# Forty projections as 20 Strassen pairs of blocks, with LayerNorm, RG-LRU and SSD between the products

## The chip, the cores and the metric

The program runs on one core of a Trainium2 chip. The metric is device time in microseconds (us); the median of three runs of the kernel before is 1493.83 us (1492.61 to 1494.31). The engines of the core are named as in the profile: PE (TensorE, matrix products), PEld (its weight loads), DVE (VectorE), ACT (ScalarE), POOL (GpSimd) and SP (SyncE, whose queue SPq issues the DMAs of this kernel).

## The reference

One layer of a hybrid encoder, for 1,024 prompt tokens and 64 tokens of a second stream, 1,088 in all, all in float32:

```python
h = rms_norm(x, norm_pre);  proj = h @ w_in          # (1088 x 1024) @ (1024 x 10248)
u_a = rg_lru(conv4(lru_x)) * silu(lru_g)             # block-diagonal gates, scan over time
u_b = rms_norm(ssd(silu(conv4(xbc)), dt) * silu(z), ssd_norm)   # chunked state-space scan
u_c = silu(layer_norm(conv31(glu(cf_in)))) * silu(cf_g)
u_d = stick_breaking_attention(q, k, v) * silu(sb_g)
y_b = u_b @ w_down[b]                                # four times 512 -> 1024
m = sum_b sigmoid(merge_b) * y_b                     # merge: 4 x 1024 columns of proj
out = x + rms_norm(m @ w_out, norm_post)
```

The columns of `w_in` make 80 blocks of 128, and 8 columns for `dt`. 32 of the 80 blocks are the merge gates, 4 each are the gates of the RG-LRU (`C_LG`) and of the convolution module (`C_CG`).

## The kernel before, in words

All products keep float32 accuracy with three passes: each operand is split in a rounded part and its remainder (`hh`, `hl` for the activations, `w_hi`, `w_lo` for the weights), and hi·hi, hi·lo, lo·hi are summed in PSUM (`mm3`, L104 to L107). Activations lie with channels on the partitions and tokens along the row, in three pieces `SPL` of 256, 384 and 448 tokens. One block of the projection (`proj`, L176) is a load of 512 KB of weights, a split on ACT (L97) and DVE (L98), and for each piece 8 x 3 = 24 matmuls, so 72 per block, with an evacuation by the caller.

PE runs in the order of the program text. The other engines' queues are in order too, their order set by a scheduler from priorities (`tc.high_priority`). `Feed` is how matrix work is laid between the steps of something else: `feed.step(n)` issues n pieces of the projections in its queue.

The stages: norm and transposes of the input (to about 35 us); the first projections; attention in 68 units with four chunks of heads (115 to 587 us), between whose units the projections of the convolution module, of q, k, v and of 12 gate blocks are fed, the latter (`spill`, L309) with a sigmoid on ACT, a product on DVE and a store to DRAM; the RG-LRU (587 to 745 us), fed with its own and the SSD's blocks and their 4-tap convolutions; the LayerNorm of the convolution module (745 to 880 us); the SSD in 9 chunks of 128 tokens (880 to 1230 us). From the LayerNorm on, the feed holds `merge(bi)` for three of the four branches: per block of the gate 72 matmuls of the projection, a sigmoid (L689), 36 matmuls with `w_down` (`down`), product and sum on DVE (L698, L699). A chunk of the SSD (`first`, `second`, `third`, `fourth`) has five feed steps in its loop. Its result is split into `uoh`, `uol` and stored (L924, L925). The last branch in `order` is the SSD's own: its 8 gate blocks are projected from 1230 to 1334 us, its downs run to 1382 us, and then the product with `w_out`. The operands of the downs are loaded by `load_u` (L662), two transfers per piece.

## Time and profile before

| | |
|---|---|
| median of the runs | 1493.83 us |
| span of the profiled execution | 1490.9 us |
| PE busy | 1460.1 us (98%) |
| DVE busy | 921.1 us (62%) |
| ACT busy | 588.5 us (39%) |
| POOL busy | 118.9 us (8%) |
| DMA, mean over the span | 97 GB/s |

The profiled execution spans 1490.9 us from its first to its last instruction; the median of the device times is 2.9 us longer. Times inside the span are counted from its start. A matmul's duration is modelled and overlaps the next one; how long PE takes for a row of matmuls is read from their starts.

### The profile page before, as it was taken

The page shows a single profiled execution, that of the slowest core. Times are in us where ns is not written, and L with a number is a line of the kernel's source. Part 1 is how long each engine was busy: PE and PEld are TensorE (multiplying, and loading weights), DVE is VectorE, ACT ScalarE, POOL GpSimd, SP SyncE. Part 2 cuts the span into 40 slices and gives each one's busy share as a digit, 9 for nine tenths or more (in the row PEclk, how much of TensorE's full clock was granted, in tenths as well). Part 3 has the DMA queues.
Part 4 walks back from the last instruction along what each step waited for, and adds up shares of the span by engine and source line. Part 5 has one row for each costly group of instructions (what it writes and reads, how often), then busy time and mean ns, then how long its engine had stood idle before and what let it go on. Part 6 is the DMA issues. An engine that isn't in the chain of part 4 may idle for free.

```text
span 1490.9 us, 23008 instructions
## 1 busy us (share of the span) xinstructions
PE 1460.1 (98%) x9157; PEld 1360.5 (91%) x9157; DVE 921.1 (62%) x1379; ACT 588.5 (39%) x1000; POOL 118.9 (8%) x157
## 2 busy tenths in 40 slices
PE   6999999999999999999999999999999999999997
PEld 5898999999999998999999999999999999999885
DVE  6289589579769955677765554656655541019433
ACT  6323434443453344666644322333332332124211
POOL 0003212231221222000000000000000000000000
PEclk9999999999999999999999999999999999999999
DMA  6232212313212323454433354222621234113322
GB/s 209 75 87 63 72 61 68 103 44 89 92 46 87 98 87 109 138 117 107 116 124 116 110 169 142 82 68 83 196 78 57 75 88 148 51 43 113 99 85 71
DMA packets 103339, 144.17 MB, mean 97 GB/s; under 512 B 20800, under 2 KB 82112, under 8 KB 103232
## 3 DMA queue, kind: packets, MB, share of 16 engines
q1 hardware_dynamic: 103232, 142.71, 31.9%
q8 instruction: 72, 1.18, 0.3%
q14 instruction: 35, 0.29, 0.1%
HBM read 97.95 MB, written 40.53 MB: 93 GB/s over the span
## 4 chain that ended last, share of the span: by engine, by line
PE 87%; issue 6%; DVE 4%; DMA 1%; ACT 1%; POOL 1%; SPq 0%; DVEq 0%; POOLq 0%; ACTq 0%
PE pj L105 24%; PE pj L106 24%; PE pj L107 24%; PE pg L468 2%; PE pg L450 2%; PE pg L106 1%; PE pg L107 1%; PE pg L105 1%; DVE cvo L239 1%; PE pz L417 1%; PE pz L418 1%; PE pg L878 1%; PE pg L736 1%; PE pg L871 1%; DMA g_bc<-in_npre_dram 0%
## 5 line engine op out<-in xcount | busy, mean ns | idle before, releaser
L105 PE MATMUL pj<-hh,w_hi 128*128 128x384 f32 (+2 forms) x1920 | 637.6, 332 | 1.7 <-ACT hh L220 1.7
L106 PE MATMUL pj<-hl,w_hi 128*128 128x384 f32 (+2 forms) x1920 | 631.8, 329 | 1.8 <-DVE hl L221 1.8
L107 PE MATMUL pj<-hh,w_lo 128*128 128x384 f32 (+2 forms) x1920 | 631.5, 329 | 0.0
L105 PEld LDWEIGHTS pj<-hh,w_hi 128*128 128x128 f32 x1920 | 363.6, 189 | 16.6 <-issue 2.1
L106 PEld LDWEIGHTS pj<-hl,w_hi 128*128 128x128 f32 x1920 | 363.7, 189 | 14.4 <-DVE hl L221 2.6
L107 PEld LDWEIGHTS pj<-hh,w_lo 128*128 128x128 f32 x1920 | 363.5, 189 | 11.0
L98 DVE TENSOR_TENSOR w_lo<-w_raw,w_hi 128x1024 fp32r<-128x1024 f32 x96 | 117.5, 1224 | 226.9 <-ACT w_hi L97 226.7
L97 ACT ACTIVATE w_hi<-w_raw 128x1024 fp32r<-128x1024 f32 x96 | 101.7, 1060 | 281.7 <-PE pj L106 262.6
L239 DVE SCALAR_TENSOR_TENSOR cvo<-cbuf,p_t,cvo 128x1118 f32<-128x1118 f32 x120 | 165.6, 1380 | 2.1
L105 PE MATMUL pj<-uh,w_hi 128*128 128x384 f32 (+2 forms) x384 | 126.2, 329 | 0.0
L107 PE MATMUL pj<-uh,w_lo 128*128 128x384 f32 (+2 forms) x384 | 126.2, 329 | 0.0
L106 PE MATMUL pj<-ul,w_hi 128*128 128x384 f32 (+2 forms) x384 | 126.1, 328 | 0.0
L438 DVE TENSOR_TENSOR_SCAN fb<-fb,ones 128x128 f32<-128x128 f32 (+8 forms) x68 | 90.0, 1324 | 38.0 <-POOL fb L435 37.4
L435 POOL TENSOR_SCALAR_AFFINE_SELECT beta<-beta 128x128 f32<-128x128 f32 (+1 forms) x72 | 78.2, 1086 | 14.4 <-ACT beta L431 13.7
L698 DVE TENSOR_TENSOR sg<-pj,sg 128x256 f32<-128x256 f32 (+2 forms) x48 | 25.7, 535 | 84.9 <-PE pj L107 80.6
L689 ACT ACTIVATE sg<-pj 128x256 f32<-128x256 f32 (+2 forms) x72 | 33.7, 468 | 112.2 <-PE pj L107 112.0
L105 PEld LDWEIGHTS pj<-uh,w_hi 128*128 128x128 f32 x384 | 72.7, 189 | 2.3
L106 PEld LDWEIGHTS pj<-ul,w_hi 128*128 128x128 f32 x384 | 72.6, 189 | 2.2
L107 PEld LDWEIGHTS pj<-uh,w_lo 128*128 128x128 f32 x384 | 72.6, 189 | 2.2
L435 POOL TENSOR_SCALAR_AFFINE_SELECT fb<-fb 128x128 f32<-128x128 f32 (+1 forms) x72 | 38.2, 530 | 449.2 <-ACT fb L430 354.4
L439 DVE TENSOR_TENSOR beta<-beta,fb 128x128 f32<-128x128 f32 (+8 forms) x68 | 50.3, 740 | 4.3 <-POOL beta L435 0.7
L452 ACT ACTIVATE wT<-pg 128x512 f32<-128x512 f32 (+3 forms) x96 | 43.3, 485 | 18.1 <-PE pg L450 17.8
(313 smaller groups left out, 1683.0 us busy)
## 6 DMA issues: line engine op xcount, KB each, us to landing
w_raw<-in_win_dram SPq DMA_DIRECT2D x80, 512.0 KB, 3.7
w_raw<-in_wdn_dram SPq DMA_DIRECT2D x16, 512.0 KB, 3.6
xt<-in_x_dram SPq DMA_DIRECT2D x8, 512.0 KB, 10.5
xbc<-xs SPq DMA_DIRECT2D x8, 512.0 KB, 2.6
xb<-xbc SPq DMA_DIRECT2D x8, 512.0 KB, 4.9
w_raw<-in_wout_dram SPq DMA_DIRECT2D x8, 512.0 KB, 3.7
xr<-in_x_dram SPq DMA_DIRECT2D x8, 512.0 KB, 3.8
out_y_dram<-yo SPq DMA_DIRECT2D x16, 256.0 KB, 2.3
```

The source lines that it names most:

```text
L97: S.activation(hi, r3, AF.Copy)
L98: V.tensor_sub(lo, r3, hi.bitcast(FT))
L105: PE.matmul(out, ah, bh, start=first, stop=False)
L106: PE.matmul(out, ah, bl, start=False, stop=False)
L107: PE.matmul(out, al, bh, start=False, stop=last)
L239: V.scalar_tensor_tensor(out[:, :n], b[:, i:i + n], w[:, i:i + 1], out[:, :n], op0=OP.mult, op1=OP.add)
L435: G.affine_select(t_[s, 1024 - w:1024], t_[s, 1024 - w:1024], pattern=[[-1, w]], compare_op=OP.is_gt, fill=fill, base=0, channel_multiplier=1)
L438: V.tensor_tensor_scan(F[:, rev], F[:, rev], ones[:, 0:1].to_broadcast([128, n]), 1.0, OP.mult, OP.mult)
L439: V.tensor_tensor(B[:, L:1024], B[:, L:1024], F[:, L + 1:1025], op=OP.mult)
L450: PE.transpose(p[:, (j - j0) * 128:(j - j0 + 1) * 128], B[:, L + j * 128:L + (j + 1) * 128], ident)
L452: S.activation(wT[:, j0:j1, :], p[:, :(j1 - j0) * 128].rearrange("p (j c) -> p j c", c=128), AF.Copy)
L689: S.activation(sg[:, :n], p[:, :n], AF.Sigmoid)
```

## The change

Forty of the 80 blocks (the 8 gate blocks of convolution module and RG-LRU, and the 32 merge gates) are no longer projected one by one: two blocks make a `Pair`, and the product of their 2 x 2 arrangement (2 halves of the inner dimension, 2 halves of 544 tokens) is made with seven products in place of eight, after Winograd. The seven weight operands are sums of 512-wide quarter blocks made on POOL (L693, L694, L695, L702), each split by ACT and DVE; the seven activation operands `quad` are made once, after the attention, with additions on POOL (L601) and DVE. One product is 2 x 12 matmuls of 272 columns. Sums of products are made by accumulating in the same PSUM bank, by ACT copies (L725) and by DVE additions (L728) in `r`, and each quarter is stored to DRAM.

So the order of the program is another: the attention is fed with the 12 blocks that have short convolutions (8 of the SSD, 4 of the RG-LRU) in place of 12 gate blocks; then come 4 blocks for z, `quad` and `dt`; then the 140 products of the 20 pairs, and after each one step of the chain LayerNorm, RG-LRU, SSD; then all downs, whose gates are loaded from DRAM. The pieces `SPL` of the remaining blocks are 384, 384 and 320 tokens, of two V blocks as before.

```diff
-SPL = ((0, 256), (256, 384), (640, 448))
+SPL = ((0, 384), (384, 384), (768, 320))
...
-    extra = [spill(C_SZ + c, sz_d[:, c]) for c in range(4)] + [spill(C_LG + c, lg_d[:, c]) for c in range(4)]
-    extra += [spill(C_CG + c, cg_d[:, c]) for c in range(4)]
+    extra = [sx_chunk(c) for c in range(8)] + [lx_chunk(c) for c in range(4)]
...
+    def short_conv(chunk, state, tail_o, w, bias, dst, silu):
+        b = conv_buf(cp, WA, KA, state, "abuf", bufs=1)
...
+            conv(xc, b, NA, KA, w, bias, first=True)
+            if silu:
+                sg = cp.tile([128, NA], FT, name="sg", tag="abuf", bufs=1)
+                S.activation(sg, xc[:, :NA], AF.Sigmoid)
+                V.tensor_tensor(xc[:, :NA], xc[:, :NA], sg, op=OP.mult)
...
+    ORDER = (1, 2, 6, 5, 7, 3, 4)
+    BANK = {1: "a", 6: "a", 7: "a", 4: "a", 2: "b", 5: "c", 3: "c"}
...
+                G.tensor_tensor(s1, a21, a22, op=OP.add)
+                G.tensor_tensor(s2, s1, a11, op=OP.subtract)
+                G.tensor_tensor(a21, a11, a21, op=OP.subtract)
...
+            for j in ORDER:
+                hi, lo = weights()
...
+                for q in range(2):
...
+                            PE.matmul(p, a_[:, k], b_[:, k, s], start=new and k == 0 and z == 0, stop=k == 3 and z == 2,
+                                      skip_group_check=True)
+                    with tc.high_priority(offset=C_PRIO):
+                        if to:
+                            S.activation(R[to][:, s], p, self.last if j == 4 else AF.Copy)
+                        else:
+                            r = R[{2: (0, 0), 7: (1, 1), 3: (0, 1)}[j]][:, s]
+                            V.tensor_tensor(r, p, r, op=OP.add)
...
+                between()
...
+    def chains():
+        yield from wait(15)
+        yield from layer_norm()
+        yield from lru()
+        yield from ssd()
...
+    for n, pair in enumerate(pairs):
...
+            next(side, None)
+        pair.run(next_weights, step)
+    while next(side, left) is not left:
+        pass
...
+    us = [load_u(0, ut, tag="u")]
+    nwd = weights(wdn[order[0], 0])
...
+    gates = [load_gate(order[0], d) for d in range(8)]
+    us += [load_u(1, hp, tag="hh"), load_u(2, hp, tag="hl")]
...
+        if bi == 1:
+            us.append(load_u(3, ut, tag="u"))
```

`layer_norm` goes through four quarters of 272 tokens, `lru` through 8 pieces of 544 tokens by one of four channel blocks, `ssd` through the 9 chunks; each `yield` hands over to one product. The chain waits 15 products, takes 23 for the LayerNorm, 34 for the RG-LRU and 77 for the SSD, 149 in all. Between two chunks of the SSD lie 8 products. What is left when the products end runs in the last loop. The tile `u0` (operands of the first downs) is in a pool on the right side, over the place of the SSD's tiles; `u1` and `u2` lie where `hh` and `hl` were, and the fourth lies in `u0`'s place.

**PE at the end of the SSD.** Before, the last chunk's state (L871), diagonal (L878) and state update (L886) stand between the matmuls of a down and those of a gate block (`Sb` is the state, `M` the decayed scores, `xdt` and `xdd` the inputs times dt, `pg` and `pj` are PSUM banks):

```order
L107 MATMUL pj<-uh_10224,w_lo 128x256
L871 MATMUL pg<-Sb_8590,xb 64x256 [waits DMAHW4_49,DMAHW3_49]
L871 MATMUL pg<-Sb_8590,xb 64x256
L878 MATMUL pg<-M_11417,xdt 64x64 [waits PE_49]
L878 MATMUL pg<-M_11417,xdt 64x64 x3
L878 MATMUL pg<-M_11418,xdt 64x64 x4
L886 MATMUL pg<-xdd,bt 64x128 [waits Activation_49]
L886 MATMUL pg<-xdd,bt 64x128 x3
L105 MATMUL pj<-hh_96,w_hi 128x384
```

After, from the same step (L955, L965, L974; L989 and L1000 are the transposes and the column sum of `join` and `norm`) to the first matmuls of the downs:

```order
L955 MATMUL pg_12633<-Sb_9644,xb 64x256 [waits DMAHW6_49,DMAHW5_49,Activation_49]
L955 MATMUL pg_12633<-Sb_9644,xb 64x256
L965 MATMUL pg_12638<-M_12576,xdt 64x64 [waits DVE_49,PE_49]
L965 MATMUL pg_12638<-M_12576,xdt 64x64 x3
L965 MATMUL pg_12638<-M_12581,xdt 64x64 x4
L974 MATMUL pg_12652<-xdd,bt 64x128 [waits DVE_49]
L974 MATMUL pg_12652<-xdd,bt 64x128 x3
L989 MATMUL pg_12663<-ident,yt 128x64 [waits DVE_49,PE_49]
L989 MATMUL pg_12663<-ident,yt 128x64 x3
L1000 MATMUL pg_12673<-yt,ones 128x64 [waits DVE_49,Activation_49]
L109 MATMUL pj_12767<-u_12692,w_hi 128x384 [waits DMAHW5_49,Activation_49]
L110 MATMUL pj_12767<-u_12692,w_hi 128x384 [waits DMAHW0_49]
```

What moved: no matmul of other work stands beside these steps any more. The 13 rows ahead of them, from the segment sums of chunk 8 (L912) on, stand behind the last product (L721) too, with no product among them.

**SP at the end of the SSD.** Before, the last stores (L924, L925) stand among the loads of operands of the last branch (L662), with weights (L92) behind:

```order
L662 DMA ul_11867<-ul_74 128x4x256 [waits DMAHW6_49,PE_49]
L662 DMA uh_11865<-uh_70 128x4x256 [waits PE_49]
L924 DMA uh_70<-uoh 512x1x64 [waits DMAHW0_49,Activation_49]
L925 DMA ul_74<-uol 512x1x64 [waits DMAHW1_49,DVE_49]
L662 DMA ul_11871<-ul_74 128x4x384 [waits DMAHW2_49,PE_49]
L662 DMA uh_11869<-uh_70 128x4x384 [waits DMAHW3_49,PE_49]
L92 DMA w_raw<-in_win_dram 128x1024 [waits DMAHW4_49,DVE_49]
L662 DMA uh_11873<-uh_70 128x4x448 [waits DMAHW5_49,DMAHW0_49,PE_49]
```

After, the last stores (L1009, L1010) stand behind the gates `sga` and most of `u1`, and the loads of `u0` (its tile number is 12692) behind them; the first waits for the landing of the second store:

```order
L1090 DMA u_12753<-ul_76 128x4x384 [waits DMAHW1_49]
L1009 DMA uh_73<-uoh 512x1x64 [waits DMAHW2_49,Activation_49]
L1010 DMA ul_77<-uol 512x1x64 [waits DMAHW3_49,DVE_49]
L1090 DMA u_12753<-ul_76 128x4x384 [waits DMAHW4_49]
L1090 DMA u_12692<-uh_75 128x4x384 [waits DMAHW3_49,DMAHW5_49,DMAHW2_49,PE_49]
L1090 DMA u_12692<-uh_75 128x4x384 [waits DMAHW6_49]
L1090 DMA u_12692<-uh_75 128x4x320 [waits DMAHW7_49]
L1090 DMA u_12692<-ul_79 128x4x384 [waits DMAHW0_49]
L1090 DMA u_12692<-ul_79 128x4x384 [waits DMAHW1_49]
```

What moved: the operands of the next matmuls, loaded around the SSD's last stores before, stand behind them.

**ACT in the RG-LRU.** Before, a weight split and an evacuation stand between the exponential (`ga`) and the hyperbolic tangent (`gr`):

```order
L620 ACT_TABLE_LOAD
L620 ACTIVATE ga<-gr,lm_6064 128x1092 [waits Activation_49]
L97 ACTIVATE w_hi<-w_raw 128x1024 [waits DMAHW1_49,PE_49]
L577 ACTIVATE abuf<-pj 128x384 [waits PE_49]
L577 ACTIVATE abuf<-pj 128x64
L621 ACTIVATE gr<-gr,lp_6065 128x1092 [waits Activation_49]
L622 ACT_TABLE_LOAD
L622 ACTIVATE gr<-gr 128x1092 [waits Activation_49]
```

After, the three functions and two weight splits stand in a row, ahead of two evacuations of a product (L725):

```order
L852 ACT_TABLE_LOAD [waits DMAHW4_49,DVE_49]
L852 ACTIVATE ga<-gr,lm_8102 128x544 [waits Activation_49]
L853 ACTIVATE gr<-gr,lp_8103 128x544 [waits Activation_49]
L854 ACT_TABLE_LOAD
L854 ACTIVATE gr<-gr 128x544 [waits Activation_49]
L228 ACTIVATE w_hi<-w_raw 128x512 [waits PE_49]
L228 ACTIVATE w_hi<-s_8335 128x512 [waits Pool_49]
L725 ACTIVATE r<-bank 128x272 [waits PE_49] x2
```

What moved: the evacuation that stood between the functions stands behind them and two weight splits.

## Rows read from the trace of the kernel before

**Rows 1.** The page: busy time of each engine, granted clock by slice, chain by engine.

```profile
PE 1460.1 (98%) x9157; PEld 1360.5 (91%) x9157; DVE 921.1 (62%) x1379; ACT 588.5 (39%) x1000; POOL 118.9 (8%) x157
...
PEclk9999999999999999999999999999999999999999
...
PE 87%; issue 6%; DVE 4%; DMA 1%; ACT 1%; POOL 1%; SPq 0%; DVEq 0%; POOLq 0%; ACTq 0%
```

**Rows 2.** Timeline of PE, a projection: start us, us, engine, line, operation, tiles, count.

```profile
1262.92 0.28 PE L105 MATMUL pj<-hh,w_hi 128*128 128x256 f32 x1
...
1265.79 0.34 PE L105 MATMUL pj<-hh,w_hi 128*128 128x384 f32 x1
...
1269.96 0.36 PE L105 MATMUL pj<-hh,w_hi 128*128 128x448 f32 x1
...
1274.91 0.28 PE L105 MATMUL pj<-hh,w_hi 128*128 128x256 f32 x1
```

**Rows 3.** PE's matmuls by form: count | busy us, mean ns | idle.

```profile
L105 PE MATMUL pj<-uh,w_hi 128*128 128x256 f32 x128 | 36.2, 283 | 0.0
...
L418 PE MATMUL pz<-kl,qs 128*128 128x320 f32 x16 | 4.8, 306 | 0.0
...
L105 PE MATMUL pj<-uh,w_hi 128*128 128x384 f32 x128 | 43.0, 336 | 0.0
```

**Rows 4.** Busy us of each engine by stretch, then granted clock, DMA share, GB/s.

```profile
215.00:341.00 126.00, 125.81 (x875) 117.86 (x873) 101.00 (x119) 54.63 (x115) 28.06 (x36) 1.00 0.24 74
880.00:1230.00 350.00, 348.43 (x2230) 328.35 (x2229) 196.06 (x373) 119.98 (x164) 0.00 (x0) 1.00 0.35 103
579.50:583.00 3.50, 3.20 (x22) 2.90 (x24) 1.26 (x4) 1.19 (x2) 2.04 (x5) 0.51 0.13 37
590.00:600.00 10.00, 10.00 (x60) 9.55 (x60) 3.94 (x18) 3.51 (x7) 0.00 (x0) 1.00 1.03 299
```

**Rows 5.** Timeline of VectorE at the end of the SSD.

```profile
1220.94 0.41 DVE L905 TENSOR_TENSOR yz<-yz,pg 128x256 f32<-128x256 f32 x1
...
1226.11 0.54 DVE L918 RECIPROCAL rs__11767<-rs__11767 128x64 f32<-128x64 f32 x1
...
1226.69 0.87 DVE L920 SCALAR_TENSOR_TENSOR yz<-yz,p_t,rs__11767 128x64 f32<-128x64 f32 x4
...
1228.09 0.43 DVE L225 TENSOR_TENSOR uol<-yz,uoh 128x256 fp32r<-128x256 f32 x1 [0.53 <-ACT uoh L224]
```

**Rows 6.** Timeline of ScalarE at the end of the SSD.

```profile
1222.32 0.42 ACT L908 ACTIVATE yt<-yz 128x256 f32<-128x256 f32 x1 [3.13 <-DVE yz L906]
...
1224.20 1.28 ACT L917 ACT_TABLE_LOAD   x1
...
1227.64 0.42 ACT L224 ACTIVATE uoh<-yz 128x256 fp32r<-128x256 f32 x1 [1.84 <-issue]
```

**Rows 7.** Groups of single operations on VectorE and ScalarE by form.

```profile
L98 DVE TENSOR_TENSOR w_lo<-w_raw,w_hi 128x1024 fp32r<-128x1024 f32 x96 | 117.5, 1224 | 226.9 <-ACT w_hi L97 226.7
...
L225 DVE TENSOR_TENSOR uol<-yz,uoh 128x512 fp32r<-128x512 f32 x8 | 5.4, 679 | 0.0
...
L772 DVE RECIPROCAL lnr<-lnr 128x256 f32<-128x256 f32 x1 | 1.7, 1746 | 0.0
...
L224 ACT ACTIVATE uoh<-yz 128x512 fp32r<-128x512 f32 x8 | 5.0, 631 | 19.8 <-PE pg L878 19.8
```

**Rows 8.** DMA issues: operation, count, KB each, median us from issue to landing.

```profile
ul<-uol SPq DMA_DIRECT2D x8, 256.0 KB, 2.7
```

**Rows 9.** Timeline of ScalarE in the RG-LRU.

```profile
704.11 1.21 ACT L621 ACTIVATE gr<-gr,lp 128x1092 f32<-128x1092 f32 x1
705.34 1.28 ACT L622 ACT_TABLE_LOAD   x1
```

**Rows 10.** Groups on POOL: an affine select beside VectorE's work and one alone.

```profile
L435 POOL TENSOR_SCALAR_AFFINE_SELECT beta<-beta 128x128 f32<-128x128 f32 (+1 forms) x72 | 78.2, 1086 | 14.4 <-ACT beta L431 13.7
...
L85 POOL TENSOR_SCALAR_AFFINE_SELECT tri_le<-ones 128x128 f32<-128x128 f32 x1 | 0.3, 292 | 0.0
```

More of the change, by code (lines that the diff above doesn't have):

```diff
@@ new lines, in encoder_step, with spill, evac @@
+    tmp = a5.enter_context(tc.tile_pool(name="tmp", bufs=1, side="right", reuse_waits="tile"))
+    def spill(chunk, dst):
+        def evac(t0, n, p):
+            g = tmp.tile([128, NM], FT, name="t3", bufs=3)
+            S.activation(g[:, :n], p[:, :n], AF.Silu)
+            dma(dst[:, t0:t0 + n], g[:, :n])
+        yield from proj(chunk, evac)
+    feed.add(*(spill(C_SZ + c, sz_d[:, c]) for c in range(4)))
+    feed.step(1)
+    tlo, thi = slice(0, HT), slice(HT, T)
+    k0, k1 = slice(0, 4), slice(4, 8)
@@ new lines, in encoder_step @@
+    feed.step(2)
+    dtr = tmp.tile([16, T], FT, name="dtr")
+    for i, (t0, n) in enumerate(SPL):
+        p = pg()
+        for k in range(8):
+            for q, hx in enumerate((hh, hl)):
+                PE.matmul(p[:16, :n], wd2[:, k, :], hx[:, k, t0:t0 + n], start=k == 0 and q == 0, stop=k == 7 and q == 1)
+        S.activation(dtr[:, t0:t0 + n], p[:16, :n], AF.Copy)
+    feed.step(3)
+    pd = pg()
+    for i in range(9):
+        r = 128 if i < 8 else 64
+        PE.transpose(pd[:r, i * 16:i * 16 + 16], dtr[:, i * 128:i * 128 + r], ident[:16, :16])
@@ new lines, in stored, with done, wait @@
+    def stored(base, c, dst, func=None):
+        def done(e, f, r, last):
+            if func and not last:
+                S.activation(r, r, func)
+            dma(dst[:, c + e, f * HT:f * HT + HT], r)
+        return Pair(base + c, base + c + 1, done, func or AF.Copy)
+    pairs = [stored(C_CG, c, cg_d, AF.Silu) for c in (0, 2)] + [stored(C_LG, c, lg_d, AF.Silu) for c in (0, 2)]
+    pairs += [stored(C_MG, 2 * i, mg_d) for i in range(16)]
+    def wait(n):
+        for _ in range(n):
+            yield
@@ new lines, in chains, with ahead @@
+    def chains():
[3 more added lines that the diff above has]
+        yield from ssd()
+    ready = []
+    todo = [(p, j) for p in pairs for j in ORDER]
+    two = []
+    def ahead(n):
+        while todo and len(ready) < n:
+            p, j = todo.pop(0)
+            p.prepare()
+            if not two:
+                t_ = wp.tile([128, 8, 128], FR, name="w_hi"), wp.tile([128, 8, 128], FR, name="w_lo")
+                two.extend([t[:, k] for t in t_] for k in (k0, k1))
+            hi, lo = two.pop(0)
+            p.parts(j, hi, lo)
+            ready.append((hi, lo))
@@ new lines, in next_weights, with step @@
+    def next_weights():
+        ahead(3)
+        return ready.pop(0)
+    side = chains()
+    left = object()
+    for n, pair in enumerate(pairs):
+        count = [0]
+        def step(n=n, count=count):
+            count[0] += 1
+            ahead(2)
+            if count[0] == 2 and n + 1 < len(pairs):
+                pairs[n + 1].prepare()
+            next(side, None)
+        pair.run(next_weights, step)
+    while next(side, left) is not left:
+        pass
+    order = (3, 0, 2, 1)
@@ L927, in encoder_step @@
-    prev = None
-    feed.step(LNB)
-    for i in range(9):
-        ch = Chunk(i)
-        ch.first()
-        if prev:
-            prev.third()
-        feed.step(2)
-        if prev:
-            prev.fourth()
-        feed.step()
-        ch.second()
-        feed.step(2)
-        prev = ch
-    prev.third()
-    feed.step()
-    prev.fourth()
-    feed.drain()
-    p3.close()
-    b = order[3]
-    us = [load_u(b, i) for i in range(3)]
-    sgp = ctx.enter_context(tc.tile_pool(name="sgp", bufs=1, side="right", reuse_waits="tile"))
@@ L985, in encoder_step @@
+    put.close()
+    ut = ctx.enter_context(tc.tile_pool(name="op", bufs=1, side="right", reuse_waits="tile"))
+    gp_bc = ut.tile([128, D], FT, name="gp_bc")
     dma(gp_bc, ap(npost, 0, [[0, 128], [1, D]]))
```

879 lines of the change are left out of this document (472 added, 407 removed).

## The prediction

> **What bounds the kernel now.** I read the page's busy times and clock first. PE is busy 98% of the span, at nine tenths of the clock or more in every slice, and the chain that ended last is PE for 87% [rows 1]. So the time is the number of columns that PE streams, by their price, plus the few places where PE stands. Next the price: in the timeline of a projection, 24 matmuls of 256 columns run from 1262.92 to 1265.79, 24 of 384 to 1269.96, 24 of 448 to 1274.91 [rows 2], that is 0.120, 0.174 and 0.206 us from start to start, and 11.99 us for a block of 72. Then the stages: in one attention chunk (215 to 341) VectorE is busy 101.0 of 126.0 us, in the SSD 196.1 of 350.0 and ScalarE 120.0, while PE has 125.8 and 348.4 [rows 4]. So nearly nothing waits today, every microsecond that PE is spared counts, and every one that it is made to wait counts too. Last the place where the change takes PE's cover away, the end of the SSD [rows 5, 6, 8].
>
> **Fewer columns (the gain).** The forty blocks cost 40 x 11.99 = 479.6 us. The change makes 20 pairs x 7 products x 24 = 3,360 matmuls of 272 columns. No row has 272. The modelled durations of 256, 320 and 384 columns are 283, 306 and 336 ns [rows 3], which is 163 and 162 ns over the pitch of 256 and 384; so 320 has a pitch of 0.144, and 272, a quarter of the way from 256 to 320, has 0.126 to 0.127. I take 0.1265: 3,360 x 0.1265 = 425.0, so -54.6. Bounds from the rows on either side: 0.120 gives 403.2 (-76.4), 0.144 gives 483.8 (+4.2). The 38 blocks left, in pieces 384, 384, 320, cost 24 x (0.174 + 0.174 + 0.144) = 11.8 against 11.99: -7.3 together. The 32 downs have half the matmuls per block: -3.1. Sum -65.0.
>
> **The end of the SSD (the largest loss).** The steps after the last product were hidden: from 1218 to 1242 us matmuls of downs and gates lay beside them. The changed order has nothing beside them, so I add them up, from T0, the end of the last product. Segment sums and exponential with a table load (1.28 [rows 6]) 2.3. Join of chunk 7: transposes 0.3, two 512-wide VectorE operations at 0.68 [rows 7], Square 0.63 [rows 7], two folds 0.7: 3.3. Norm of chunk 7: ones matmul 0.3, table load 1.28 and root 0.4 [rows 6], reciprocal 0.95 (1.746 for 256 [rows 7]), four scalings 1.4 (half as wide they took 0.87 [rows 5]), `uoh` 0.63, `uol` 0.68 [rows 7]: 5.5. That is T0 + 11. `xdt` of chunk 8 takes the place of `uoh`, so it waits for the store: 2.7 [rows 8], T0 + 13.8; scaling 0.7, diagonal 1.1, `yz` 0.9: 16.5. Join of chunk 8, 64 wide: 0.41 for each of two operations [rows 5], Square 0.42 [rows 6], folds 0.5 and a transpose: 18.3. Its norm, read from 1224.20 (table load) to the end of `uol` at 1228.09 + 0.43 [rows 5, 6], 4.3 less a short wait for ScalarE's turn: T0 + 22.
>
> Then the loads. The first down needs `u0` high and low of the first 384 tokens; its six loads are issued behind the SSD's last store, and that store stands behind gates and `u1`, 2.8 MB in the queues. At 299 GB/s, the most that a stretch of the trace moved [rows 4], these take 9.3 us from about T0 + 18 on, so the stores land near T0 + 28 and `u1`'s next piece at 30. The first low piece is the fourth load: 2.95 MB, 9.9 us at 299, so PE has its second matmul near T0 + 41. PE's own small matmuls in that stretch, 4 us, were there before too: +37. It would be 25 if the queues were empty at T0 + 20 (store 2.7, two pieces at 299) and the chain two steps ahead; 50 if loads and stores shared half the rate. I take 37, the sum of the rows.
>
> **What follows an idle PE.** After PE stood idle from 577 to 579.5 its granted clock was 0.51 for 3.5 us [rows 4], the lower level (1.2 GHz), then full. An idle stretch of 30 us ends the same way: 1.8 us lost there, and about 1 for the two later pieces of `u0`: +3. Bounds 0 and 6.
>
> **Between the products.** Per quarter of the LayerNorm (5 products, 15.2 us, and two float32 sums, 0.9) VectorE has 7,072 elements in its own steps at 1.224 us per 1,024 [rows 7] = 8.5, a reciprocal of 272 at 1.8 [rows 7], five weight splits at 0.68, four or five additions of 0.43 [rows 5], overheads of 0.1 each: 16.1 of 16.1 us. Per piece of the RG-LRU (4 products and 12 gate matmuls, 13.7 us) ScalarE has three table loads of 1.28 [rows 6], four gates at 0.45, three functions and two splits of 544 at 0.66 (0.63 for 512 [rows 7]), four weight splits at 0.63 and 4 to 5 evacuations at 0.42 [rows 6]: 13.4 of 13.7. Two queues with nothing to spare: I put 1 us per quarter and 1 to 1.5 per piece, 14. The SSD has slack (VectorE 23 of 29.7 us per chunk by the same prices), less a `uoh` store that lands 0.8 us before `xdt` needs it: 5, and 2 at pair boundaries. Of this 21, some 12 us stood in 600 to 1230 before: so much do PE's starts there leave over their pitches, of which busy time, whose ends are modelled, shows 1.6 in the SSD [rows 4]. +9. Bounds 0 and 40.
>
> On POOL the changed kernel has four 512-wide additions per pair, which the trace lacks. An affine select of 128 columns took 0.29 us alone and 1.09 beside VectorE's work [rows 10], so 512 wide I bound it by 1.2 and 4.3 us: 5 to 17 of the 21 us of a pair, prepared a pair ahead, at no cost. The Trainium skill ("GPSIMD Engine Reference", 3.1 and the specifications in 1) gives about 2.6 cycles per element for an operation of two tensors, some 1.1 us here as an estimate, and says that the engine shares SBUF's interface with VectorE operations of two SBUF inputs. By that VectorE would lose up to 3.2 us per LayerNorm quarter, where it has none, and the sum would be 13 us higher. The slow selects beside VectorE agree with the sharing; which side pays, the rows of before show for POOL alone.
>
> **Attention.** Twelve blocks with convolutions add 3 operations of 1,092 (1.38 to 1.22, [rows 7] for 1,024) or some 4 us per block to VectorE, and 1.3 more for a SiLU, less the 1.6 of a gate block: 40 us in 470, so 111 of 126 us per chunk. VectorE keeps its cover; the buffer `abuf` is single, so a second such block in a row waits for the first's convolution, 3 PSUM banks (12 us) ahead. +5, bounds 0 and 15. The start of the products (PSUM pools change, first quarter operands): +1.
>
> **Sum.** 1490.9 - 65.0 + 37 + 3 + 9 + 5 + 1 = 1480.9; with the 2.9 us between span and median, 1483.8: 1484.
>
> **Rivals.** *ScalarE's queue bounds the RG-LRU* (slower than before). Two table loads, three functions and two weight splits in a row, 5.8 us, stand ahead of two evacuations. A bank is accumulated into again one product later, so PE has 3.0 to 4.5 us; what is past that, and the splits queued behind, PE waits. If PE stands for the row less half a product, 4.3 us in each of 8 pieces, that is 35 us: 1519 with the rest as above. It decides from 1.6 us per piece (13 us) on. For it: 13.4 of 13.7 us. Against: table loads and functions come when the gates are there, often with the evacuation already done; in the trace ScalarE waits for PE, not the other way.
>
> *Table switches cost double* (slower). In the RG-LRU a table load started 0.02 us after the tangent's end, 704.11 + 1.21 to 705.34 [rows 9]: no wait ahead of it. If each of the 24 loads in the 8 pieces had a wait of its own length ahead, ScalarE would need 13.4 + 3 x 1.28 = 17.2 of 13.7 us, +28: 1512. The Trainium skill ("ScalarE: Activation LUTs", What ACT_TABLE_LOAD costs) states that much: 1,283 ns and a drain of 1,380 ns for every switch. By that rule the time would be 1515, as an estimate; the trace agrees with the first figure and not with the second.
>
> *A shorter end.* The scheduler's order is no promise of when the queues empty: with gates and `u1` landed before chunk 8's stores, `u0` starts at T0 + 24 and needs only its first pieces: 20 us rather than 37, 1467.
>
> *The saving isn't there.* If 272 columns cost what 320 do, the products take 483.8 us, nothing is saved, and the time is 1542.
>
> **How the numbers follow.** The forecast 0.57; ScalarE's queue 0.18; double switches 0.04; shorter end 0.17; no saving 0.04. The forecast's own range is 1466 to 1502, mainly the end (25 to 50) and the products (9, up to 20). With the rivals, 8 in 10 lie between 1460 and 1517. A measurement of this kernel can tell about 0.2% (3 us). Faster by more, under 1490.8: 0.7 of the forecast and the shorter end, 0.57. Within: 0.2 of the forecast, 0.12. Slower: the rest, 0.31.
>
> **What would show it.** Right: 3,360 matmuls at 0.126 to 0.127 from start to start; one gap of PE of some 35 us, from about 1140 on in the new span (downs 189 us and the last product with the output, 108 us, behind it), ended by DMA of `u0`, with the half clock behind it; VectorE over 95% busy in the LayerNorm, ScalarE in the RG-LRU; nearly no gaps in the SSD. Wrong: gaps of 3 us and more in each RG-LRU piece ended by ScalarE, gaps ended by POOL at pair starts, a clock at the lower level in the products, or a last stretch of under 20 us.

## The result, and the profile after

The changed kernel takes 1519.49 us (median, 1519.28 to 1520.43) against 1494.0 in the same comparison: a ratio of 1.0174 with a 95% interval of 1.0162 to 1.0186, 25 us slower. The forecast was 1484 with a range up to 1517. One of the runs below, of the kernel with later loads, took 4903.67 us and is left out. The profiled execution spans 1518.6 us, 27.7 more than before. Three parts of the page of after, busy time, granted clock by slice and chain, answer to [rows 1]:

```profile
PE 1417.0 (93%) x9665; PEld 1352.7 (89%) x9665; DVE 1060.6 (70%) x1604; ACT 676.1 (45%) x1227; POOL 262.4 (17%) x245
...
PEclk9999999999999999999898999999999589999999
...
PE 43%; DVE 6%; DMA 4%; ACT 4%; issue 1%; SPq 0%; DVEq 0%; ACTq 0%
```

PE is busy 43.1 us less, since columns were saved. But the span holds 70.8 us more in which PE is not busy, PE's share of the chain is 43% where it was 87%, and one slice is at half the clock. PE's waits of after from 640 to 1240 us, by line and releaser (total, times, longest), say where PE stands. In before, 600 to 1230 holds 1.1 us of such waits; here it is 66:

```profile
PE pg L779 <- DVE lns L756: 14.9, 3, 6.7
PE pj L109 <- DMA u<-uh: 13.8, 1, 13.8
PE pg L965 <- DVE xdt L937: 8.0, 4, 5.5
PE pj L110 <- DMA u<-ul: 6.4, 1, 6.4
PE pg L1000 <- DVE yt L995: 6.3, 2, 3.6
PE pg L109 <- ACT bdah L228: 6.3, 1, 6.3
PE bank L721 <- ACT r L725: 3.0, 5, 1.1
```

The LayerNorm's column sums (L779) take 14.9, the first gate matmul of the RG-LRU (L109 by `bdah`) 6.3, and the rows with `u`, `yt` and most of `xdt` are the end of the SSD. Over the whole trace the waits with a releaser are 93.8 us, 22.3 before. By place: end of the SSD 35.1, LayerNorm 14.9, RG-LRU 10.5, SSD between products 4.1, start of the products 7.2, attention from 467 us on 5.0 (2.9 before); the rest is the head of the program, as before.

The windows of after, with PE's busy time (second figure), granted clock, DMA share and GB/s at the end of each row, answer to [rows 4]. The first is a stretch of products, the next three follow a wait of PE in the LayerNorm or at the start of the RG-LRU, the last three are the end of the SSD:

```profile
650.40:707.80 57.40, 57.39 (x457) 57.39 (x458) 21.68 (x38) 22.34 (x47) 14.71 (x11) 1.00 0.37 124
...
735.00:740.00 5.00, 3.51 (x13) 3.28 (x14) 2.93 (x5) 3.26 (x4) 0.00 (x0) 0.50 0.84 256
...
780.00:785.00 5.00, 4.47 (x23) 4.24 (x24) 2.74 (x3) 0.49 (x1) 0.17 (x1) 0.65 0.38 109
805.00:810.00 5.00, 4.95 (x22) 4.63 (x22) 0.88 (x7) 1.78 (x4) 0.00 (x0) 0.50 0.15 46
1174.40:1212.40 38.00, 9.25 (x56) 6.08 (x55) 14.62 (x35) 19.96 (x24) 0.00 (x0) 0.57 0.94 309
1212.40:1219.40 7.00, 0.62 (x2) 0.22 (x2) 0.00 (x0) 0.00 (x0) 0.00 (x0) 0.50 1.07 372
1219.40:1225.00 5.60, 5.60 (x20) 5.60 (x21) 0.56 (x1) 0.00 (x0) 0.00 (x0) 0.60 1.07 366
```

Three readings. 457 matmuls of 272 columns in 57.40 us are 0.1256 each, so 3,360 cost 422, where 425 was forecast. From the last product (1174.4) to the second matmul of the downs (1219.4) 45 us pass, with DMA at 0.94 to 1.07 of its engines. And PE ran at or near the lower clock level (1.2 GHz) behind waits in five places after the attention, not one: busy time times what is missing of the clock is 1.8, 1.6, 2.5, 4.0, 0.3 and 2.2 us in these rows, with 740 to 745 (0.74) and 620 to 625 (0.50) 2.7 more, 15 us in all. Summed in stretches of 5 us over the whole trace it is 18.2, against 2.7 before, so 15 to 16 are new. Without it PE's busy time would have fallen by 58, not 43. So the account is -58 for PE's work at full clock, +15 for clock, +71.5 for waits: +28.5, against a measured +27.7.

The cause of the largest wait between products stands in the timeline of after, at the second quarter of the LayerNorm (start, duration; in brackets idle time and releaser):

```profile
729.05 1.12 ACT L228 ACTIVATE lnh<-lnx 128x1088 fp32r<-128x1088 f32 x1 [1.19 <-DVE lnx L789]
...
730.19 0.58 SPq L793 DMA_DIRECT2D uh<-lnh  x1
...
734.09 1.11 ACT L775 ACTIVATE lnq<-lnx 128x1088 f32<-128x1088 f32 x1 [1.56 <-DMA uh<-lnh]
735.22 1.28 ACT L781 ACT_TABLE_LOAD   x1
735.24 0.72 DVE L755 TENSOR_TENSOR lns<-lnq 128x544 f32<-128x544 f32 x1 [2.19 <-ACT lnq L775]
...
735.99 0.44 DVE L756 TENSOR_TENSOR lns<-lns 128x272 f32<-128x272 f32 x1
...
736.49 1.28 PE L779 MATMUL pg<-lns,ones 128*128 128x272 f32 x2 [6.06 <-DVE lns L756]
```

The result `lnh` of one quarter and the squares `lnq` of the next have one place. So the square waits until the store of `lnh` has landed (730.19 to 734.09), the folds wait for the square, PE for the folds. No engine is full here; it is a row of latencies through one buffer.

### The profile page after: what moved, and what is told of

It reads as the page before. It is cut to its first block, busy times and chain, and to the rows that moved or that the text cites. A ratio compares the mean times of both kernels' runs of the same rounds, so it can differ in the third digit from the quotient of the medians.

```text
span 1518.6 us, 24934 instructions
## 1 busy us (share of the span) xinstructions
PE 1417.0 (93%) x9665; PEld 1352.7 (89%) x9665; DVE 1060.6 (70%) x1604; ACT 676.1 (45%) x1227; POOL 262.4 (17%) x245
## 4 chain that ended last, share of the span: by engine, by line
PE 43%; DVE 6%; DMA 4%; ACT 4%; issue 1%; SPq 0%; DVEq 0%; ACTq 0%
PE bank L721 19%; PE pj L110 7%; PE pj L111 7%; PE pj L109 7%; DVE w_lo L229 1%; DMA sga<-mgs 1%; ACT w_hi L228 1%; DMA u<-ul 1%; DMA uh<-uoh 1%; DMA ul<-uol 1%; DVE gx L860 1%; ACT L852 1%; PE pg L965 0%; DMA uh<-lnh 0%; PE pg L912 0%
## 5 line engine op out<-in xcount | busy, mean ns | idle before, releaser
L109 PE MATMUL pj<-hh,w_hi 128*128 128x384 f32 (+3 forms) x960 | 317.8, 331 | 6.7 <-ACT t L584 5.4
L110 PE MATMUL pj<-hl,w_hi 128*128 128x384 f32 (+3 forms) x960 | 315.3, 328 | 1.6 <-DVE hl L225 1.6
L111 PE MATMUL pj<-hh,w_lo 128*128 128x384 f32 (+3 forms) x960 | 315.1, 328 | 0.0
L721 PE MATMUL bank<-hh,w_hi 128*128 128x272 f32 x640 | 191.8, 300 | 3.2 <-ACT t L584 1.8
L109 PEld LDWEIGHTS pj<-hh,w_hi 128*128 128x128 f32 x960 | 182.2, 190 | 9.5 <-ACT t L584 5.5
L721 PE MATMUL bank<-hl,w_hi 128*128 128x272 f32 x640 | 186.8, 292 | 0.0
L721 PE MATMUL bank<-hh,w_lo 128*128 128x272 f32 x640 | 186.8, 292 | 0.0
L110 PEld LDWEIGHTS pj<-hl,w_hi 128*128 128x128 f32 x960 | 182.1, 190 | 3.6 <-DVE hl L225 2.5
L111 PEld LDWEIGHTS pj<-hh,w_lo 128*128 128x128 f32 x960 | 181.9, 189 | 0.2
L721 PE MATMUL bank<-Th,w_hi 128*128 128x272 f32 x480 | 141.3, 294 | 1.5 <-ACT r L725 1.5
L109 PE MATMUL pj<-u,w_hi 128*128 128x384 f32 (+1 forms) x384 | 126.3, 329 | 13.8 <-DMA u<-uh 13.8
L721 PE MATMUL bank<-Th,w_lo 128*128 128x272 f32 x480 | 138.4, 288 | 0.0
L721 PE MATMUL bank<-Tl,w_hi 128*128 128x272 f32 x480 | 138.2, 288 | 0.0
L110 PE MATMUL pj<-u,w_hi 128*128 128x384 f32 (+1 forms) x384 | 126.4, 329 | 6.4 <-DMA u<-ul 6.4
L721 PEld LDWEIGHTS bank<-hh,w_hi 128*128 128x128 f32 x640 | 123.3, 193 | 5.5 <-ACT t L584 2.0
L721 PEld LDWEIGHTS bank<-hl,w_hi 128*128 128x128 f32 x640 | 123.1, 192 | 0.8
L721 PEld LDWEIGHTS bank<-hh,w_lo 128*128 128x128 f32 x640 | 122.8, 192 | 0.0
L101 ACT ACTIVATE w_hi<-w_raw 128x1024 fp32r<-128x1024 f32 x56 | 59.4, 1061 | 113.6 <-PE pj L110 106.5
```

Of the source, the lines that this page charges most:

```text
L101: S.activation(hi, r3, AF.Copy)
L109: PE.matmul(out, ah, bh, start=first, stop=False)
L110: PE.matmul(out, ah, bl, start=False, stop=False)
L111: PE.matmul(out, al, bh, start=False, stop=last)
L721: PE.matmul(p, a_[:, k], b_[:, k, s], start=new and k == 0 and z == 0, stop=k == 3 and z == 2, skip_group_check=True)
```

## The experiments

All are edits of the kernel after, except the last. Ratios are to the kernel before; after itself has 1.0174.

**One product less per chunk of the SSD.** The chain takes 149 steps and there are 140 products, so nine steps are left when they end. With 7 products between two chunks the chain is 8 shorter.

```diff
-            yield from wait(2)
+            yield
```

> The changed kernel with one edit: after the diagonal step of an SSD chunk the chain hands over to one product in place of two, so 7 products lie between two chunks, not 8, and the last chunk's steps stand among the last products. The end from the last product to the second matmul of the downs took 45.0 us in the changed kernel. Theory A (half of that end is the SSD chain without a product beside it, the other half the load of u0 behind its last store): the end shrinks to 20 to 25 us, the time falls by 20 to 25 us to about 1497. Rival B (VectorE, 23 us per chunk by prices, is the bound once a chunk has 26 us instead of 30): PE waits 2 us or more in each chunk, and the time falls by less than 8 us, to 1512 or more.

Measured: 1518.19, ratio 1.0162 (1.0147 to 1.0177). The gap at the end fell from 45.0 to 21.1 us, as the first theory had it, but the time did not follow. The matmuls of the last chunk now lie in front of the gap, the SSD between products waits 9.9 us where it was 4.1 (`xdt` 4.5, `lt` 5.1), and the downs, whose loads collide sooner, wait 4.8 for their weights. The products end 14.6 us later and the downs take 7 us longer, which took back 22 of the 24 us. Theory A had the gap right and rival B the time; rival B's 2 us of waits in each chunk were not there, so neither held whole.

**Places of their own for the LayerNorm's results.**

```diff
-            gh = ln.tile([128, 4, QT], FR, name="lnh", tag="lnq")
-            gw = ln.tile([128, 4, QT], FR, name="lnl", tag="lng")
+            gh = ln.tile([128, 4, QT], FR, name="lnh")
+            gw = ln.tile([128, 4, QT], FR, name="lnl")
```

> The changed kernel with one edit: the split result of a LayerNorm quarter (lnh, lnl) has tiles of its own in place of those of the squares and the gates (lnq, lng). PE stands 14.9 us in the LayerNorm of the changed kernel and runs at the lower clock behind two of its stalls. Theory A (the quarter's chain of latencies is what PE waits for: the next Square waits for the landing of lnh's store, the gates wait for lnl's): the stalls fall to 3 us or less, the lower clock goes too, and the time falls by 12 to 20 us, to 1500 to 1507. Rival B (VectorE's sum of 16.1 us per quarter is the bound): the stalls stay over 10 us and the time falls by less than 5 us.

Measured: 1507.89, ratio 1.0091 (1.0076 to 1.0106): 11.6 us from two lines. The LayerNorm's waits fell from 14.9 to 4.5, in these rows of PE's waits from 640 to 1240 us:

```profile
PE pg L772 <- DVE lns L756: 2.7, 1, 2.7
...
PE pg L779 <- DVE lns L756: 1.7, 2, 0.9
```

So the shared place was the main cause, as read, and VectorE's sum of work was not. The gain is just under the 12 to 20 us expected; the wait at the start of the RG-LRU grew from 6.3 to 7.9.

**The first operands in six tiles of their own.** `u0` lies over the quarter operands instead of over the SSD's tiles, in pieces, so that its first tokens can be loaded before the SSD ends. Only the core of the edit:

```diff
-    us = [load_u(0, ut, tag="u")]
     nwd = weights(wdn[order[0], 0])
     a1.close()
+    ut = ctx.enter_context(tc.tile_pool(name="ut", bufs=1, reuse_waits="tile"))
+    us = [Parts(0)]
```

> The changed kernel with one edit: the operands of the first downs (u0) lie where the seven products' quarter operands were, in six tiles, and the gates sga lie on the right side over the SSD's tiles; the last SSD steps stay behind the last product. Theory A (the first downs wait for u0's load, which starts at the SSD's last store only for the sake of its place): the wait for u0, 20 us of PE's idle time at the end, falls to 3 us or less, the SSD's steps (25 us) stay, and the time falls by 15 to 20 us to about 1502. Rival B (the queues are full anyway, u0 shares them with the gates and u1): the downs wait for gates or u1 instead, and the time falls by less than 8 us.

Measured: 1515.2, ratio 1.0136 (1.0119 to 1.0152). The end went from 45.0 to 25.3 us, and a new wait ended 38 us later: PE waits for the second weights of the downs (L101 is their rounding on ScalarE). PE's waits from 1160 to 1420 us:

```profile
PE pj L109 <- ACT w_hi L101: 13.5, 1, 13.5
PE pg L965 <- DVE xdt L937: 6.4, 1, 6.4
```

The loads ahead of the second weights are the same by the program; only what PE waits for changed, as rival B had it.

**The operand sums on VectorE.** The eight additions of 1,088 columns that make `quad` (L601) go from POOL to VectorE.

```diff
-            G.tensor_tensor(g, hh[:, ks, t].bitcast(FT), hl[:, ks, t].bitcast(FT), op=OP.add)
+            V.tensor_tensor(g, hh[:, ks, t].bitcast(FT), hl[:, ks, t].bitcast(FT), op=OP.add)
```

> The changed kernel with one edit: the eight additions of 1,088 elements that rebuild the activations for the quarter operands run on VectorE, not on POOL. PE stands 5.4 us there (an evacuation by ScalarE is queued behind a split that waits for POOL and VectorE) and has the lower clock behind it, 63.4 us from the attention's end to the first product for 56 us of matmuls. Theory A (POOL's two-tensor additions, 3 us alone, and the slower VectorE beside them are the cause): the stall goes, and the time falls by 5 to 8 us to about 1513. Rival B (VectorE's own eight splits and eight subtractions are the chain, and additions there lengthen it by 10 us): the time stays within 2 us or rises.

Measured: 1516.12, ratio 1.0146 (1.0128 to 1.0164). The products start 7.9 us sooner (642.5 for 650.4) and the 7.2 us of waits there become 1.8. Of that 3.4 us are left in the median, and since the four runs scatter from 1512.28 to 1518.48, the gain in time is not clear. What was wrong with POOL shows in after, POOL's and VectorE's timelines from 587 us on:

```profile
588.28 14.66 POOL L601 TENSOR_TENSOR g<-hh,hl 128x1088 f32<-128x1088 f32 x5
...
611.10 2.33 POOL L695 TENSOR_TENSOR w_raw<-w_raw,w_raw 128x512 f32<-128x512 f32 x1
613.39 6.00 POOL L601 TENSOR_TENSOR g<-hh,hl 128x1088 f32<-128x1088 f32 x2
```

```profile
612.21 2.38 DVE L229 TENSOR_TENSOR Tl<-g,Th 128x1088 fp32r<-128x1088 f32 x1
...
626.77 1.29 DVE L229 TENSOR_TENSOR Tl<-g,Th 128x1088 fp32r<-128x1088 f32 x1
```

An addition of 1,088 took POOL 2.9 us in the mean of the first five: 2.5 us where VectorE stood (at 616.93) and up to 3.6 beside it. The same subtraction on VectorE took 2.38 us at 612.21, while POOL added, and 1.29 at 626.77, when POOL stood.

**The weight sums on VectorE.** The four additions of 512 per pair (L693, L694, L695, L702) go the same way.

```diff
-                G.tensor_tensor(s1, a21, a22, op=OP.add)
+                V.tensor_tensor(s1, a21, a22, op=OP.add)
...
-                    G.tensor_tensor(a, a, self.src[6], op=OP.subtract)
+                    V.tensor_tensor(a, a, self.src[6], op=OP.subtract)
```

> The changed kernel with one edit: the four 512-wide sums and differences of a pair's weight blocks run on VectorE, not on POOL. In the changed kernel's trace a POOL operation takes 1.28 us alone and up to 2.8 beside VectorE, and VectorE's 544-wide fold takes 0.73 us alone and 1.81 beside POOL. Theory A (POOL and VectorE hold each other up by about as much as the work itself would cost VectorE, 4 x 0.68 us per pair): the time stays within 4 us of 1519. Rival B (POOL's work is free for VectorE): VectorE gets 2.7 us per pair more, 2 us per LayerNorm quarter where it is full, and the time rises by 6 to 15 us. Rival C (the sharing costs more than the work): the time falls by over 4 us.

Measured: 1520.34, ratio 1.0168 (1.0151 to 1.0185), no change, as theory A had it. It is the plainest measure of the sharing: 80 additions at 0.686 us are 55 us of new work for VectorE, but its busy time rose by only 11.7 (1060.6 to 1072.3), while POOL's fell by 121 (262.4 to 141.2). POOL's additions had cost VectorE 43 us. Since VectorE bounds little here, it made no difference.

**Later loads of `u1` and `u2`.** They are issued when the second and sixth down are done instead of with the gates.

```diff
-    us += [load_u(1, hp, tag="hh"), load_u(2, hp, tag="hl")]
...
+                if bi == 0 and i == 0 and d in (1, 5):
+                    late = hp.tile([128, 2, 4, T], FR, name=f"u{len(us)}", tag="hh" if d == 1 else "hl")
...
+                    us.append(load_u(len(us), None, late))
```

> The changed kernel with one edit: the operands u1 and u2 are loaded only when the second and the sixth block of the first branch's downs are done (one column of each of their pieces is first written from those results), so they don't stand in the queues ahead of the SSD's last stores and of u0. Theory A (the last part of the end is traffic: 2.8 MB of gates and u1 stand ahead of the stores): the end of 45.0 us falls to about 36, the time by 7 to 10 us to about 1511. Rival B (the end is set by the SSD's chain and u0's own 3 MB): within 3 us of 1519, or slower if the second branch then waits for u1.

Measured: 1520.65 (median of 1517.8, 1520.65 and 1523.38), ratio 1.0178 (1.0159 to 1.0197), span 1516.0: no gain. The end shrank by only 4.5 us (45.0 to 40.5), and the downs took 196.9 us where they took 192. The eight gates, 4.4 MB, still stand in front.

**Four edits at once** (7 products, places of their own, `u0` in pieces, operand sums on VectorE).

> The edits of the first four experiments together: 7 products per SSD chunk, own tiles for the LayerNorm's results, u0 where the quarter operands were and gates on the right, activation sums on VectorE. Theory A (the end has two halves in a row, the SSD's steps and u0's load, so each edit alone only uncovers the other, and what starts earlier runs into the wall of 17 MB of loads): PE's gap at the end falls under 5 us, but the first branch's second pair of weights is late behind the gates and operands as in the experiment with u0 on the left (13 us there): about 1485 to 1490. Rival B (the single gains add: 1.3 + 11.6 + 4.3 + 3.4): 1499.

Measured: 1503.33, ratio 1.0064 (1.0049 to 1.0079), slower than either theory's number. The gap at the end is gone: 1169.4 to the second down at 1171.3. Instead the downs take 221.9 us in place of 192. PE's longest wait from 1160 to 1400 us, and SP's queue in that stretch (the rows are issues of DMAs):

```profile
PE pj L109 <- ACT w_hi L101: 22.6, 1, 22.6
```

```profile
1176.41 6.30 SPq L1120 DMA_DIRECT2D sga<-mgs  x8
1183.62 6.30 SPq L1088 DMA_DIRECT2D u<-uh  x3
...
1202.19 6.44 SPq L1088 DMA_DIRECT2D u<-ul  x3
1208.73 2.78 SPq L1120 DMA_DIRECT2D sga<-mgs  x3
1211.57 0.49 SPq L96 DMA_DIRECT2D w_raw<-in_wdn_dram  x1
```

PE took up the downs at 1171 and stood for the second weights from 1202 on. SP issued them only at 1211.57, since eight gates, `u1`, `u2` and three more gates stood ahead in the same queue.

**The loads in another order**, on top of the four edits: later `u1` and `u2` as above, the downs' weights asked for one block earlier, and other waits of the RG-LRU's chain (4 and 1 for 2 and 3).

```diff
-        yield from wait(2)
+        yield from wait(4)
...
-                if i == 0 and d % 2 and (d < 7 or bi < 3):
+                if i == 0 and d % 2 == 0 and (d < 6 or bi < 3):
```

> The four edits together, with three more: u1 and u2 loaded late as in the experiment for that, the weights of the downs loaded one block earlier, and two products more before the RG-LRU's first step (two fewer behind its last). Theory A (with the traffic spread, nothing but PE's own work and the SSD's slack is left): 1468 to 1476, faster than the kernel before by over 1%. Rival B (the downs are bound by loads of 43 MB in 190 us): PE waits for gates or operands throughout the downs, 1485 or more.

Measured: 1498.71, ratio 1.0031 (1.0019 to 1.0042), not the 1468 to 1476 hoped for. The weights' longest wait is down from 22.6 to 8.1 us. The other waits of the chain were no gain: 4.6 by `xg` at the RG-LRU's start, and `lt` in the SSD rose from 5.5 to 8.5 us.

**Fetching ahead on the same queue**, on top of the last: two weights ahead of the gates, `u1` and `u2` still later (fourth and eighth down), the LayerNorm's input a quarter sooner.

```diff
+    nw2 = weights(wdn[order[0], 1])
+    raws = [fetch(wdn[order[0], 2])]
     gates = [load_gate(order[0], d) for d in range(8)]
+    raws.append(fetch(wdn[order[0], 3]))
...
-                if bi == 0 and i == 0 and d in (1, 5):
+                if bi == 0 and i == 0 and d in (3, 7):
```

> The seven edits with two more: the first branch's weights are fetched ahead of its gates (the loads of u1 and u2 two blocks later still), and a LayerNorm quarter's input is loaded a quarter ahead. In the version before this PE waits 10.2 us for weights in the downs and 5.1 for a LayerNorm input. Theory A (they stand behind 4.4 MB of u1 and gates that wait for VectorE, in a queue in order): both waits go with the lower clock behind them, 1498.7 - 15 to 20: 1479 to 1484. Rival B (the DMA engines are full, not the queue's order at fault): the waits turn up at other loads, 1493 or more.

Measured: 1505.61, ratio 1.0073 (1.0056 to 1.009), worse. The wait moved to 1263.53 and is 16.5 us: now weights of the second branch, issued at 1251.74, stand behind a gate and the operands `u2` and `u3` of the third and fourth branch, issued on the same queue from 1232.09 on. That is rival B's number; whether full DMA engines are its reason, as rival B says, the next run decides.

**Another queue for the weights.** The four edits, later `u1` and `u2`, weights one block earlier, and from the second pair of blocks on the downs' weights on POOL's DMA queue; the RG-LRU's waits as in after.

```diff
-    def weights(src):
+    def weights(src, put=dma):
         raw = wp.tile([128, 1024], FT, name="w_raw", bufs=2)
-        dma(raw, src)
+        put(raw, src)
...
-                    nwd = weights(wdn[b, d // 2 + 1] if d < 7 else wdn[order[bi + 1], 0])
+                    nwd = weights(wdn[b, d // 2 + 1] if d < 6 else wdn[order[bi + 1], 0], nc.gpsimd.dma_start)
```

> The changed kernel with the first four edits, u1 and u2 loaded late (after the second and sixth block), the downs' weights fetched a block earlier and, from the second pair on, through POOL's DMA queue, which has nothing else to do there; the RG-LRU's waits as in the changed kernel. With the weights in SP's queue PE waited 22.6, 10.2 and 16.8 us for them in the three versions before. Theory A (the weights waited for their place in a queue in order, not for bandwidth): the wait in the downs is under 2 us, and the time is 1478 to 1486, faster than the kernel before. Rival B (loads of 17 MB at 370 GB/s fill the DMA engines whatever the queue): over 8 us of waits in the downs, 1492 or more.

Measured: 1482.02 (1478.44 to 1482.72), ratio 0.9911 with an interval of 0.9894 to 0.9927: faster than both kernels. Of its trace: the page's busy times, two of POOL's issues of weights, a window of the downs, and PE's largest waits from 640 to 1400 us:

```profile
PE 1413.6 (95%) x9665; PEld 1348.7 (91%) x9665; DVE 1061.0 (72%) x1616; ACT 672.2 (45%) x1225; POOL 245.9 (17%) x252
```

```profile
1176.07 0.53 POOL L96 DMA_DIRECT2D w_raw<-in_wdn_dram  x1 [7.01 <-DVE w_lo L102]
1197.75 0.53 POOL L96 DMA_DIRECT2D w_raw<-in_wdn_dram  x1 [21.15 <-DVE w_lo L102]
```

```profile
1205.00:1215.00 10.00, 10.00 (x63) 10.00 (x63) 3.81 (x6) 1.06 (x1) 0.53 (x1) 1.00 1.06 385
```

```profile
PE pg L109 <- ACT bdah L228: 8.1, 1, 8.1
PE pg L912 <- DVE lt L902: 5.1, 6, 1.1
PE pg L965 <- DVE xdt L937: 4.8, 3, 2.7
PE pj L110 <- DMA u<-ul: 4.6, 2, 3.5
```

No row with `w_hi` is left, though the DMA engines are as full as before (385 GB/s, share 1.06): the weights had waited for their turn, not for bandwidth. Waits are 59.2 us over the trace, PE busy 46.5 us less than before and idle with a releaser 36.9 more, which is 9.6 of the 9.9 us of span gained. How much the queue alone gives isn't separated from the RG-LRU's waits: between this and the kernel with the other load order lie 16.7 us, of which 10.2 are waits for weights (8.1 the longest) and 3.4 waits for `lt` in the SSD.

**Eight plain products per pair** in the changed order, without any of the sums: what the order costs without the method.

```diff
-    ORDER = (1, 2, 6, 5, 7, 3, 4)
+    ORDER = (1, 2, 3, 4, 5, 6, 7, 8)
...
-            self.src = {1: a11, 6: s2, 2: a12, 7: a21, 5: s1, 4: a22, 3: a12}
+            self.src = {1: a11, 2: a12, 3: a21, 4: a22, 5: a11, 6: a12, 7: a21, 8: a22}
```

> The changed kernel's order of work with plain products: a pair of blocks is made with eight products of halves that accumulate two by two, no sums of operands on POOL and VectorE, no quarter operands; all else stays. 160 products in place of 140. Theory A (Winograd's saving is real and is spent by the order around it): 20 more products of 24 x 0.1263 us are +60.6; the SSD's steps and u0's load (40 us of the end) come beside the 11 products behind the chain, -35 to -40; the stall at the quarter operands goes, -8: 1525 to 1540, 30 to 45 us over the kernel before, which is what the new order alone costs. Rival B (the seven products themselves, with their sums and evacuations, are what lost the time): 1500 or less.

Measured: 1521.05, ratio 1.0174 (1.0158 to 1.0189), the same as the changed kernel, and just under theory A's 1525 to 1540. Its page and its largest waits from 640 to 1420 us:

```profile
PE 1466.9 (97%) x10145; PEld 1406.0 (93%) x10145; DVE 961.6 (63%) x1488; ACT 672.3 (44%) x1228; POOL 113.4 (7%) x157
```

```profile
PE pg L750 <- DVE lns L727: 6.5, 3, 2.6
PE pj L109 <- ACT w_hi L101: 5.4, 1, 5.4
PE pg L109 <- ACT bdah L228: 5.1, 1, 5.1
```

The order alone costs 27 us in the median; in the span, 28.8 more, it is 22.6 of waits and 6.8 of PE. Its 160 products are more than the 149 steps of the chain, so the end of the SSD is covered (1.6 us), where the 140 products of the changed kernel leave it bare. So the eighth of the products that was saved was also the cover of the chain's last steps. Against the changed kernel it has 480 matmuls of 272 columns more, 60.3 us, but 49.0 us less of waits (44.9 for 93.9) and 11.5 us less lost to the clock (6.7 for 18.2, summed as above). That is the whole of what the seven products save: the waits around them and the clock behind the waits took it back.

**The pieces alone, in the kernel before**: 384, 384 and 320 tokens for 256, 384 and 448.

```diff
-SPL = ((0, 256), (256, 384), (640, 448))
+SPL = ((0, 384), (384, 384), (768, 320))
```

> The kernel before with one part of the change alone: token pieces of 384, 384 and 320 (the first two V blocks keep 256, 384, 448), nothing else. By the pitches read from the trace (0.120, 0.174, 0.206 us for 256, 384, 448 columns, 0.144 for 320) a block of 72 takes 11.81 us in place of 11.99, a block of downs 5.90 in place of 6.00. Theory A (PE's columns are the time, 98% busy): 78 x 0.19 + 32 x 0.10 = 18 us less: 1474 to 1479. Rival B (smaller last pieces leave less time for evacuations and the LayerNorm's and SSD's steps): half of it or less, 1484 and more.

Measured: 1494.84, ratio 1.0003 (0.9993 to 1.0012), no change, against theory A; it is rival B's number. Its timeline of PE at the first matmul of each piece, with the one behind (384 follows 384):

```profile
1263.41 0.31 PE L105 MATMUL pj<-hh,w_hi 128*128 128x320 f32 x1
...
1266.92 0.34 PE L105 MATMUL pj<-hh,w_hi 128*128 128x384 f32 x1
...
1275.27 0.31 PE L105 MATMUL pj<-hh,w_hi 128*128 128x320 f32 x1
```

24 matmuls of 320 took 3.51 us, 0.146 each, not 0.144, and a block 11.86 us, not 11.81 against 11.99 [rows 2]. By that the columns are worth 12 us in all. But PE's busy time fell by 3.2 us only, and waits rose by 6.0, with 3.9 for `w_lo` and 2.7 for `xg` among them, both of VectorE.

## Why the prediction was wrong

*Fewer columns*: the price of 272 columns, taken between rows, was right (422 against 425). The two smaller terms, -7.3 and -3.1, were too large: they rested on 0.144 for 320 columns, read from modelled durations, where a line through the pitches of 256 and 384 gives the 0.147 that was about measured; the run of the pieces alone shows the gain of a block at 0.13 us rather than 0.19, so -4.9 and -2.1, and none of it in the time. In sum the columns are worth -64.6, as forecast. PE's busy time at full clock fell by 58 only. Most of the rest is starts that come behind their pitch while the modelled end of the matmul ahead still covers them, so that no gap shows: summed over the large matmuls, with the measured pitches, these are 18 us from 640 to 1174 in after, 8 of them clock, against 5 from 600 to 1230 in before (and 11 there in the run of the pieces alone). The prediction had no term for them.

*The end of the SSD*: the mechanism was right, loads of `u0` behind gates and `u1`, and the size a little low, 45.0 us from the last product to the second down for a forecast of 41. The run with `u0` in pieces shows that 20 of it were those loads.

*Between the products*, +9: this is the step that failed, in two places. First, the allowance of 12 us that "stood in 600 to 1230 before" and was taken off was not there to take: before has 1.1 us of waits there and 5 us of late starts, and in after the late starts did not give way to the new waits but grew. Without the allowance the sum would have been 1496, no change. Second, the LayerNorm was priced as a sum of VectorE's work, 16.1 of 16.1 us, at 1 us a quarter. VectorE was busy 71.7 of 96.2 us from 707.8 to 804, not 95% and more; PE waited 14.9 us for a chain through a shared buffer and a store, and two lines took 10.4 of them away. The RG-LRU's 8 to 12 (10.5 measured) and the SSD's 5 (4.1) were near, though 6.3 of the RG-LRU's came once, at its start. In all 29.4 us of waits stand here for +9, inside the bounds of 0 and 40.

*What follows an idle PE*, +3: the rule was right and counted once; it applied in five places after the attention and cost 15. Each new wait of 5 to 7 us cost 1.4 to 3 more behind it.

*Start of the products*, +1: 7.2, since POOL made the operand sums at 2.9 us each and slowed the splits of VectorE. *Attention*, +5: 2.1 of waits more. From the first scores (at 113.7, before 115.3) to the last (573.7, before 573.6) it took 1.7 us longer, so the term was small, as forecast, and somewhat too large.

The misses add up: +7 in PE's work at full clock, +12 for clock, +20 between the products (29.4 for 9), +6 at the start, -2 at the end of the SSD by its waits (35 for 37), -3 in attention: 40, less 1.3 for a shorter wait at the head and the 1.1 that stood there before, against 37.7 us between the forecast span of 1480.9 and 1518.6.

*The rivals.* ScalarE's queue in the RG-LRU gave 1519 as its number, which is where the time came out, and it was not the cause: PE's waits for the evacuations (`r`, L725) are 3.0 us in five places, the longest 1.1, not 35, and ScalarE was busy 86.3 of the 106 us from 804 to 910, with time to spare. A right number from a wrong place, so its match is luck. The doubled table switches fell: at 735.22 above a table load begins 0.02 us after the activation ahead of it ends (734.09 + 1.11). If the drain that the Trainium skill states for every switch ("ScalarE: Activation LUTs", What ACT_TABLE_LOAD costs) stood ahead of the load, it would have begun 1.4 us later; the trace disagrees. The shorter end needed empty queues, and they ran at 309 to 372 GB/s throughout. The saving itself was there.

*POOL.* Its additions of 512, bounded by 1.2 and 4.3 us, took 1.29 us where POOL worked alone and up to 2.8 beside VectorE. Both engines pay for working side by side: VectorE lost 43 us to the weight sums. That did not make the time, as the run with these sums on VectorE shows: VectorE had it to spare. The Trainium skill ("GPSIMD Engine Reference", 3.1 and the specifications in 1) speaks of a shared SBUF interface, and the trace agrees; its cycle count gives 1.1 us as an estimate for such an addition, against 1.29 measured.

What stays open: how much of the 27 us that the changed order costs could be mended with eight plain products too. Its waits, 22.6 us more than before, and 4 us more of lost clock are what could be given back, so as an estimate it would come to 1494 to 1498, and the seven products, at 1482 when mended, would still be ahead; the mended plain order itself was not run.

## What to carry to other kernels

When matrix work is made shorter, count the steps that hid behind it: here 140 products had to cover 149 steps. Price a tight stage not by adding up each engine's work but by following one round through its buffers, stores and loads from one matmul to the next, and give each wait of 5 us and more some 2 us of slow clock on top, as measured here (1.4 to 3). When a burst of loads is moved, look at what stands behind it in its queue: a small load that is needed soon belongs on another queue.
